# Stick-breaking attention in a hybrid decoder layer: two heads at a time in plain float32, each on one half of the array, in place of one head at a time in split float32r

## The chip, the cores and the metric

The kernel runs on one core of a Trainium2 chip. The metric is the device time of one execution in microseconds. Three executions of the kernel before took 1371.71, 1368.38 and 1372.44 us; the median is 1371.71 us. One more execution was recorded by the profiler; all durations below come from that one.

## The reference

One layer of a decoder trunk, 1024 tokens of width 1024, everything in float32. What the change touches is the attention half: 8 heads of 64 features.

```python
h = _modulate(_rmsnorm(x, norm1_g[l]), sh1, sc1)
p = h @ w_in[l]                       # q, k, v (512 each) and u (512)
q = _rmsnorm(q, q_norm_g[l]); k = _rmsnorm(k, k_norm_g[l])   # per head
o_attn = _stick_breaking(q, k, v)
o_ssm = _s5(u, ...)
o = concatenate([_rmsnorm(o_attn, attn_out_g[l]), _rmsnorm(o_ssm, ssm_out_g[l])])
x = x + g1 * (o @ w_out[l])
h = _modulate(_rmsnorm(x, norm2_g[l]), sh2, sc2)
up = _causal_dwconv(h @ ffn_w_up[l], ffn_conv_w[l], ffn_conv_b[l])
x = x + g2 * ((gelu(gate) * val) @ ffn_w_down[l])

def _stick_breaking(q, k, v):         # for each query t and key s < t
    z = einsum('bhqd,bhkd->bhqk', q, k) / sqrt(64)
    log_1m = where(mask, log_sigmoid(-z), 0.0)
    tail = cumsum(log_1m, reverse=True) - log_1m
    w = where(mask, exp(log_sigmoid(z) + tail), 0.0)
    return einsum('bhqk,bhkd->bhqd', w, v)
```

The weight of key s is sigmoid(z) times the product of sigmoid(-z) over the keys between s and the query.

## The kernel before

The program has three phases. **Phase A** makes norm1 and the modulation, the input projection of `u`, the state-space half (`ssm_batch`), and q, k and v. **Phase B** is attention head by head, with the output projections laid between. **Phase D** is the gated MLP (`upps`, `dnps`).

*Order.* Instructions are written in the order of the code, and a scheduler then reorders them on each engine by a timeline that it works out itself, as far as buffers and dependences allow. Each engine then runs its list in order. Weight loads stand on TensorE too (PEld in the profile) and overlap with the matmuls ahead of them. Loads and stores are issued on SP's queue, the stores of q and k (`qk_d`) on ACT's.

*Split operands.* Most products are made in float32r, and an operand that must keep all its bits is split in two: a rounded copy (`hi`, `wh`) and the remainder (`lo`, `wl`), made by a subtraction. So a projection is three matmuls a block (L551 to L553, and L773 to L775 for the output projection `wops`).

*q, k and v (L591 to L647).* For each 128 tokens the projections leave a PSUM bank `o`; q and k are normalised, transposed on PE into the one bank `qkT` (L613), and copied by ACT into the first half of `hl` (rounded to float32r); DVE writes the remainder into the second half. Both halves go to DRAM, `qk_d[cix, r]`. v is split in the same way into `vt`, 64 columns of hi and 64 of lo a head, and goes to `v_d`. `hl` and `vt` share two buffers of 512 KB. `ada_back` (`ada_acc`, L67, and `adps`) runs between them: it makes the modulation rows for later from the `ada_raw` loads.

*Attention (`head`, L676).* A head has 8 query tiles of 128; tile i needs keys 0 to 128(i+1), cut into blocks of up to 512 (`zcuts`). `q1` holds hi over lo on the 128 rows, `q2` lo over hi, `k1` hi over lo, so that L694 and L695 give all four products with 128 rows each. L697 adds -1e30 to the diagonal block by a bfloat16 matmul of `nmask`. Then:

- ACT makes `nb` = sigmoid(-z/8) and `sig` = sigmoid(z/8) (L698, L699),
- DVE scans `nb` from the right as a running product (L700),
- POOL multiplies `sig` by the shifted `nb` (L702; helpers are recorded at L61),
- PE transposes the weights in groups of up to four into a bank `wT` (L707), of which there are TB = 3,
- ACT copies them as `wh` (L711), DVE subtracts to `wl` (L712, recorded at L61).

After two query tiles, L717 and L718 multiply `wh` and `wl` by `vsb` (hi and lo of v, 128 columns): 256 tokens, result in a bank `ops` of its own. Its two halves (v hi, v lo) are added: ACT copies one into `otmp` (L720), DVE adds (`oT`, L721).

*Fillers.* `after_tile` counts the attention work done, and where its share passes an entry of `marks` (L812) the next piece of the output projection of the state-space half is written into the program (`fillers`). The last head has the groups of query tiles in reverse order, and behind each the output projection of the attention half (`tail_proj`).

*State-space products.* The trace of before shows matmuls on half an array there. L488 (`vps`) writes alternately the lower and the upper 64 partitions of its result, by 64 weight columns each, from all 128 rows. The products `yps` (L506 to L514) go

```python
for pr_ in range(2):
    for q in range(4):
        # L512: 128 rows      L513, L514: the 64 rows s_ of half pr_ alone
```

The scheduler moves the first L512 and L513 of `pr_` = 1 to the front, so that on PE's list these three follow one another: L513 of `pr_` = 0, q = 3; L514 of `pr_` = 0, q = 3; L514 of `pr_` = 1, q = 0.

## Time and profile before

| what | value |
|---|---|
| median of three runs | 1371.71 us (1368.38 to 1372.44) |
| span of the profiled execution | 1365.3 us |
| instructions | 16015 |
| PE busy | 1261.6 us, 92% of the span |
| PEld busy (beside PE) | 1034.5 us, 76% |
| DVE busy | 953.0 us, 70% |
| POOL busy | 385.3 us, 28% |
| ACT busy | 375.6 us, 28% |

The profiled execution has no device time of its own beside its span; the median is 6.4 us above the span. Busy times are shares of the whole span, which has stages with different limits: q, k and v and the state space until about 338 us, attention from there to about 640 us, the MLP to the end. A matmul's row gives its start and a modelled end; matmuls are pipelined, so the duration is longer than the distance from start to start, and that distance is what one costs in a stream. Plain float32 matmuls leave two records each, float32r and bfloat16 ones a single record. "x4" in a row stands for four records run together.

### The profile page before, as it was taken

Reading aid. Unit: us, or ns where it says so; the run is one execution under the profiler, and the core shown is the slowest. Engines: PE = TensorE matmul, PEld = TensorE weight load, DVE = VectorE, ACT = ScalarE, POOL = GpSimd, SP = SyncE. Lnnn points to the kernel's source line nnn. Section 1 sums busy time; section 2 is a strip of 40 time slices with the busy share of each in tenths; the row PEclk is TensorE's granted clock in tenths of the full one; section 3 lists DMA queues with packets and bytes.
Section 4 is the critical chain, followed back from the end, with each engine's and each line's share of the span. In section 5 each row is a group of like instructions: output and inputs, shape, how many; then the busy total and the mean of one; then the engine's idle time right before and its main releaser. Section 6 shows DMA issues by size and latency. Waiting matters only on the chain.

```text
span 1365.3 us, 16015 instructions
## 1 busy us (share of the span) xinstructions
PE 1261.6 (92%) x5988; PEld 1034.5 (76%) x5988; DVE 953.0 (70%) x1465; ACT 375.6 (28%) x651; POOL 385.3 (28%) x369
## 2 busy tenths in 40 slices
PE   5979899898778996898999999999999999999998
PEld 4767778677557785676788888888888888888886
DVE  6999999873998889875775555455465655555555
ACT  5431233431765666444111101010101010101010
POOL 3562461530684449512130101111111111111100
PEclk9889889999889998898999999999999999999999
DMA  8452445657934663000620102020211111111103
GB/s 342 149 139 63 122 142 141 157 169 230 242 97 145 213 187 106 32 16 20 199 91 31 62 31 78 16 77 18 75 42 56 46 57 47 47 47 47 47 1 123
DMA packets 98264, 134.78 MB, mean 99 GB/s; under 512 B 33414, under 2 KB 66310, under 8 KB 97164
## 3 DMA queue, kind: packets, MB, share of 16 engines
q1 hardware_dynamic: 81292, 125.38, 29.5%
q10 hardware_dynamic: 16896, 8.39, 2.2%
q8 instruction: 47, 0.77, 0.2%
q14 instruction: 29, 0.24, 0.1%
HBM read 107.40 MB, written 25.17 MB: 97 GB/s over the span
## 4 chain that ended last, share of the span: by engine, by line
PE 64%; DVE 20%; DMA 7%; issue 3%; POOL 2%; ACT 2%; SPq 1%; DVEq 0%; ACTq 0%; POOLq 0%
PE upps L916 11%; PE upps L917 11%; PE upps L918 11%; PE dnps L1004 6%; PE dnps L1005 6%; PE dnps L1003 6%; DVE ada_acc L67 3%; DMA ada_raw<-in_ada_r_dram 3%; DVE nb L700 2%; PE wops L773 2%; PE wops L774 1%; PE wops L775 1%; POOL sig L61 1%; DVE st L61 1%; DMA x<-in_x_dram 1%
## 5 line engine op out<-in xcount | busy, mean ns | idle before, releaser
L916 PE MATMUL upps<-h2hi,uphi 128*128 128x512 f32 x704 | 275.5, 391 | 2.3 <-DVE cv L67 2.0
L917 PE MATMUL upps<-h2lo,uphi 128*128 128x512 f32 x704 | 274.6, 390 | 0.2 <-DVE h2lo L61 0.2
L918 PE MATMUL upps<-h2hi,uplo 128*128 128x512 f32 x704 | 274.4, 390 | 0.0
L953 ACT ACTIVATE cv<-upps,cols_sb 128x1024 f32<-128x1024 f32 x44 | 53.2, 1209 | 500.3 <-PE upps L918 500.3
L916 PEld LDWEIGHTS upps<-h2hi,uphi 128*128 128x128 f32 x704 | 132.4, 188 | 30.8 <-issue 2.8
L917 PEld LDWEIGHTS upps<-h2lo,uphi 128*128 128x128 f32 x704 | 132.4, 188 | 28.1 <-DVE h2lo L61 0.5
L918 PEld LDWEIGHTS upps<-h2hi,uplo 128*128 128x128 f32 x704 | 132.4, 188 | 27.6 <-issue 0.2
L61 DVE TENSOR_TENSOR uplo<-upraw,uphi 128x1024 fp32r<-128x1024 f32 x44 | 55.5, 1262 | 127.1 <-POOL uphi L161 127.1
L1004 PE MATMUL dnps<-wdlo,ahi 128*128 128x512 f32 x352 | 137.0, 389 | 0.9 <-DVE wdlo L61 0.9
L1003 PE MATMUL dnps<-wdhi,ahi 128*128 128x512 f32 x352 | 136.6, 389 | 0.6 <-POOL wdhi L161 0.6
L1005 PE MATMUL dnps<-wdhi,alo 128*128 128x512 f32 x352 | 136.9, 389 | 0.0
L161 POOL TENSOR_SCALAR uphi<-upraw 128x1024 fp32r<-128x1024 f32 x44 | 47.5, 1080 | 281.1 <-PE upps L917 200.0
L61 DVE TENSOR_TENSOR xs<-dnps,xs 128x512 f32<-128x512 f32 x88 | 60.9, 692 | 86.9 <-PE dnps L1005 86.9
L67 DVE SCALAR_TENSOR_TENSOR cv<-upps,cols_sb,cv 128x1023 f32<-128x1023 f32 x88 | 112.4, 1278 | 11.6 <-ACT cv L953 10.9
L61 POOL TENSOR_TENSOR sig<-sig,nb 128x127 f32<-128x127 f32 (+3 forms) x64 | 98.2, 1542 | 70.5 <-DVE nb L700 47.4
L700 DVE TENSOR_TENSOR_SCAN nb<-nb 128x128 f32<-128x128 f32 (+3 forms) x64 | 105.8, 1667 | 8.0 <-ACT nb L698 7.6
L67 DVE SCALAR_TENSOR_TENSOR ada_acc<-ada_raw,c_sb,ada_acc 128x256 f32<-128x256 f32 (+1 forms) x97 | 74.2, 779 | 24.5 <-DMA ada_raw<-in_ada_r_dram 21.2
L551 PE MATMUL qkvp<-w_hi,hhi 128*128 128x512 f32 x192 | 78.5, 410 | 3.4 <-DVE qssq L604 2.9
L552 PE MATMUL qkvp<-w_lo,hhi 128*128 128x512 f32 x192 | 78.5, 409 | 0.6 <-POOL w_lo L61 0.6
L553 PE MATMUL qkvp<-w_hi,hlo 128*128 128x512 f32 x192 | 78.0, 406 | 0.0
L1004 PEld LDWEIGHTS dnps<-wdlo,ahi 128*128 128x128 f32 x352 | 66.1, 188 | 15.0 <-DVE wdlo L61 1.3
L1003 PEld LDWEIGHTS dnps<-wdhi,ahi 128*128 128x128 f32 x352 | 65.9, 188 | 14.7 <-POOL wdhi L161 1.0
(240 smaller groups left out, 2370.7 us busy)
## 6 DMA issues: line engine op xcount, KB each, us to landing
upraw<-in_w_up_dram SPq DMA_DIRECT2D x44, 512.0 KB, 3.2
ada_raw<-in_ada_r_dram SPq DMA_DIRECT2D x48, 256.0 KB, 2.8
wdraw<-in_w_down_dram SPq DMA_DIRECT2D x22, 512.0 KB, 3.8
ada_raw<-in_ada_a_dram SPq DMA_DIRECT2D x8, 1024.0 KB, 9.3
qk_d<-hl ACTq DMA_DIRECT2D x32, 256.0 KB, 2.8
q<-qk_d SPq DMA_DIRECT2D x32, 256.0 KB, 5.7
w_raw<-in_w_qkv_dram SPq DMA_DIRECT2D x24, 256.0 KB, 3.9
xt<-in_x_dram SPq DMA_DIRECT2D x8, 512.0 KB, 5.5
```

The source lines that it names most:

```text
L61: eng.tensor_tensor(out=out, in0=a, in1=b, op=op)
L67: dve.scalar_tensor_tensor(out=out, in0=a, scalar=s, in1=b, op0=op0, op1=op1)
L551: pe.matmul(o, lhsT=lh, rhs=his[k], start=(k == 0), stop=False)
L552: pe.matmul(o, lhsT=lh, rhs=los[k], start=False, stop=False)
L553: pe.matmul(o, lhsT=ll, rhs=his[k], start=False, stop=(k == NK - 1))
L700: dve.tensor_tensor_scan(out=nb[:, 0:n][:, ::-1], data0=nb[:, 0:n][:, ::-1], data1=nb[:, 0:n][:, ::-1], initial=1.0, op0=MUL, op1=ALU.bypass)
L916: pe.matmul(o, lhsT=hi[:, k, :], rhs=rh, start=(k == 0), stop=False)
L917: pe.matmul(o, lhsT=hi[:, k, :], rhs=rl, start=False, stop=False)
L918: pe.matmul(o, lhsT=lo[:, k, :], rhs=rh, start=False, stop=(k == NK - 1))
L1003: pe.matmul(o, lhsT=hi[:, a], rhs=whi[:, b], start=(i == 0), stop=False)
L1004: pe.matmul(o, lhsT=hi[:, a], rhs=wlo[:, b], start=False, stop=False)
L1005: pe.matmul(o, lhsT=lo[:, a], rhs=whi[:, b], start=False, stop=(i == len(ops) - 1))
```

## The change

Two heads are taken at a time, and q, k, v and the weights stay plain float32 without a split. q and k of the pair lie on the 128 rows, head 0 on rows 0 to 63 and head 1 on rows 64 to 127, so a score matmul uses 64 rows of the array. In the value product each head uses 64 columns and all 128 rows, and the two heads' results lie in the two halves of one bank. The mask is now made of two bfloat16 matmuls a head on 64 rows each (`msel`, `mrow`), whose tables `mask_tables` makes in phase A. `wT` has two banks in place of three, z four in place of two; `ops` has no bank of its own and shares the two of `wops` (`mm`). Copies out of `wT` go to ACT for head 0 and to DVE for head 1. The marks end at 0.75 in place of 0.875. The diff also removes comments, which is left out here.

```diff
-    qk_d = dram.tile([2, 2, 512, 1024], F32, name="qk_d")
+    qk_d = dram.tile([2, 512, 1024], F32, name="qk_d")
-    v_d = dram.tile([1024, 8, 128], F32, name="v_d")
+    v_d = dram.tile([1024, 512], F32, name="v_d")
...
+    def mask_tables():
+        for r in range(2):
+            c = slice(r * 64, r * 64 + 64)
+            o = slice((1 - r) * 64, (1 - r) * 64 + 64)
+            pool.memset(msel[r][:, o], 0.0)
+            tt(pool, msel[r][:, c], ident_b[:, 0:64], ident_b[:, 64:128], ADD)
+            twice = const.tile([128, 2, 64], BF16, name=f"mtw{r}")
+            pool.tensor_copy(twice, ident_b[:, c].unsqueeze(1).to_broadcast([128, 2, 64]))
+            ps = psU.tile([128, 512], F32, tag="aux", name="mps2")
+            pe.matmul(ps[:, 0:128], lhsT=twice.rearrange("p a b -> p (a b)"), rhs=nmask, start=True, stop=True)
+            act.activation(out=mrow[r], in_=ps[:, 0:128], func=AF.Copy)
...
-    TB, ZB, MB = 3, 2, 2
+    TB, ZB, MB = 2, 4, 2
...
-                hl = stg.tile([128, 2, 512], F32R, tag="hl", name="hl", bufs=2)
+                hl = stg.tile([128, 512], F32, tag="hl", name="hl", bufs=3)
                 if cix == 0:
-                    act.activation(out=hl[:, 0], in_=tp, func=AF.Copy, scale=gqk)
-                    stt(hl[:, 1], tp, gqk, hl[:, 0].bitcast(F32), MUL, SUB)
+                    act.activation(out=hl, in_=tp, func=AF.Copy, scale=gqk)
                 else:
-                    act_copy(hl[:, 0], tp)
-                    tt(dve, hl[:, 1], tp, hl[:, 0].bitcast(F32), SUB)
-                for r in range(2):
-                    act.dma_start(out=qk_d[cix, r].rearrange("(a p) t -> p a t", p=128)[:, :, t * 128:(t + 1) * 128],
-                                 in_=hl[:, r].bitcast(F32).rearrange("p (a t) -> p a t", t=128))
+                    act_copy(hl, tp)
+                act.dma_start(out=qk_d[cix].rearrange("(a p) t -> p a t", p=128)[:, :, t * 128:(t + 1) * 128],
+                              in_=hl.rearrange("p (a t) -> p a t", t=128))
...
-    def head_load_qk(hd):
-        q1, q2, k1 = [qp.tile([128, 1024], F32R, tag=n_, name=n_, bufs=2) for n_ in ("q1", "q2", "k1")]
-        for dst, w, sw in ((q1, 0, 0), (k1, 1, 0), (q2, 0, 1)):
-            for r in range(2):
-                sp.dma_start(out=dst[r * 64:r * 64 + 64].bitcast(F32), in_=qk_d[w, r ^ sw, hd * 64:hd * 64 + 64, :])
-        return q1, q2, k1
+    def pair_load_qk(pr):
+        qk = [qp.tile([128, 1024], F32, tag=n_, name=n_, bufs=2) for n_ in ("q", "k")]
+        for w in range(2):
+            sp.dma_start(out=qk[w], in_=qk_d[w, pr * 128:(pr + 1) * 128, :])
+        return qk
...
-        vt = stg.tile([128, 8, 128], F32R, tag="hl", name="vt", bufs=2)
-        act.activation(out=vt[:, :, 0:64], in_=o, func=AF.Copy)
-        tt(dve, vt[:, :, 64:128], o, vt[:, :, 0:64].bitcast(F32), SUB)
-        vlast = sp.dma_start(out=v_d[t * 128:(t + 1) * 128], in_=vt.bitcast(F32))
+        vt = stg.tile([128, 512], F32, tag="hl", name="vt", bufs=3)
+        act.activation(out=vt, in_=o, func=AF.Copy)
+        vlast = sp.dma_start(out=v_d[t * 128:(t + 1) * 128], in_=vt)
...
-    def head(hd, stk, groups, after_tile, after_group):
+    def pair(pr, stk, groups, after_tile, after_group):
...
+            wts = [[ap_.tile([128, 4, 256], F32, tag="wt", name="wt", bufs=6) for _ in range((ns + 3) // 4)] for h in range(2)]
...
-                    here[0] = pe.matmul(z[:, 0:cn], lhsT=q1[:, lq], rhs=k1[:, c0:c0 + cn], start=True, stop=False)
-                    pe.matmul(z[:, 0:cn], lhsT=q2[:, lq], rhs=k1[:, c0:c0 + cn], start=False, stop=not last)
+                    for h in range(2):
+                        here[0] = pe.matmul(z[h][:, 0:cn], lhsT=q[hs[h], lq], rhs=k[hs[h], c0:c0 + cn], start=True, stop=not last)
                     if last:
-                        pe.matmul(z[:, cn - 128:cn], lhsT=ident_b, rhs=nmask, start=False, stop=True)
+                        for r in range(2):
+                            for h in range(2):
+                                pe.matmul(z[h][:, cn - 128:cn], lhsT=msel[r][hs[h]], rhs=mrow[r][hs[h]], start=False, stop=(r == 1))
...
-                    act.activation(out=wh[:, 0:jn, cs_], in_=tv, func=AF.Copy)
-                    tt(dve, wl[:, 0:jn, cs_], tv, wh[:, 0:jn, cs_].bitcast(F32), SUB)
+                        if h == 0:
+                            act.activation(out=wv, in_=tv, func=AF.Copy)
+                        else:
+                            dve.tensor_copy(wv, tv)
...
-            o = psZ.tile([128, 512], F32, tag="o", name="ops", bufs=1)
+            o = psM.tile([128, 512], F32, tag="mm", name="ops", bufs=MB)
             for s in range(ns):
-                pe.matmul(o[:, 0:256], lhsT=vt[:, s, :], rhs=whs[s // 4][:, s % 4, :], start=(s == 0), stop=False)
-                pe.matmul(o[:, 0:256], lhsT=vt[:, s, :], rhs=wls[s // 4][:, s % 4, :], start=False, stop=(s == ns - 1))
-            tmp = ap_.tile([64, 256], F32, tag="otmp", name="otmp")
-            act.activation(out=tmp, in_=o[64:128, 0:256], func=AF.Copy)
-            tt(dve, oT[h * 64:(h + 1) * 64, pr, g * 256:(g + 1) * 256], o[0:64, 0:256], tmp, ADD)
+                for h in range(2):
+                    pe.matmul(o[hs[h], 0:256], lhsT=vt[:, s, hs[h]], rhs=wts[h][s // 4][:, s % 4, :], start=(s == 0), stop=(s == ns - 1))
+            act.activation(out=oT[:, pr, g * 256:(g + 1) * 256], in_=o[:, 0:256], func=AF.Copy)
...
-    marks = [a + (b - a) * j / n for a, b, n in ((0.02, 0.14, 22), (0.14, 0.80, 24), (0.80, 0.875, 12)) for j in range(n)]
+    marks = [a + (b - a) * j / n for a, b, n in ((0.02, 0.12, 22), (0.12, 0.69, 24), (0.69, 0.75, 12)) for j in range(n)]
```

How the scheduler's order moves is shown at two places. Before, TensorE's order in the middle of the attention stage has the scores of one head (L694, L695), the mask (L697) and then a piece of the output projection (`wops`); a number behind a name tells buffers apart.

```order
L694 MATMUL z_4138<-k1_3769,q1_3767 128x512
L695 MATMUL z_4138<-k1_3769,q2_3768 128x512
L697 LDWEIGHTS ident_b_74
L697 MATMUL z_4138<-nmask_76,ident_b_74 128x128
L773 MATMUL wops_4043<-wohi_3195,ohi_3899 128x512
```

In TensorE's order after the change, in the same stage, the scores of head 0 (`z_4245`) and of head 1 (`z_4246`) come one after the other, with masks between, and then the value products of the halves (`ops`); k and q are the pair's, and z's name tells the head.

```order
L707 MATMUL z_4245<-k_3635,q_3634 128x512
L711 LDWEIGHTS msel0_81
L711 MATMUL z_4245<-mrow0_83,msel0_81 128x128
L711 LDWEIGHTS msel1_82
L711 MATMUL z_4245<-mrow1_84,msel1_82 128x128
L707 MATMUL z_4246<-k_3635,q_3634 128x512
L711 LDWEIGHTS msel0_81
L711 MATMUL z_4246<-mrow0_83,msel0_81 128x128
L711 LDWEIGHTS msel1_82
L711 MATMUL z_4246<-mrow1_84,msel1_82 128x128
L735 MATMUL ops_4063<-wt_3936,vsb_3097 64x256
L735 MATMUL ops_4063<-wt_3934,vsb_3097 64x256
```

So the scheduler put the masks of head 0, which the code writes behind the scores of both heads, ahead of the scores of head 1. A little earlier in the same order, transposes (L723) stand between the two heads' scores as well.

```order
L707 MATMUL z_4208<-k_3635,q_3634 128x384
L711 LDWEIGHTS msel0_81
L711 MATMUL z_4208<-mrow0_83,msel0_81 128x128
L711 LDWEIGHTS msel1_82
L711 MATMUL z_4208<-mrow1_84,msel1_82 128x128
L723 MATMUL wT_4037<-ident_66,sig_4011 128x128 x4
L707 MATMUL z_4209<-k_3635,q_3634 128x384
L711 LDWEIGHTS msel0_81
L711 MATMUL z_4209<-mrow0_83,msel0_81 128x128
L711 LDWEIGHTS msel1_82
L711 MATMUL z_4209<-mrow1_84,msel1_82 128x128
L723 MATMUL wT_4043<-ident_66,sig_4011 128x128 x4
```

The full-array transposes part the two half-array blocks here. Counted over the whole order of the stage, of 48 pairs of score blocks (18,432 columns a head) 21 have the heads side by side (9,344 columns), 15 have only masks between (4,736) and 12 have other work between (4,352); the value products stand in 31 runs, and full-array and half-array shapes change places 154 times.

DVE's order before, in the late part of the attention stage, has the subtractions for `wl`, the additions for `oT` and the scans of one head (named `SCALAR_TENSOR_TENSOR nb` in this listing) between each other.

```order
L61 TENSOR_TENSOR wl_4894<-wT_4954,wh_4892 128x4x128
L61 TENSOR_TENSOR wl_4996<-wT_5009,wh_4995 128x128
L700 SCALAR_TENSOR_TENSOR nb_5082<-nb_5082 128x512
L61 TENSOR_TENSOR wl_4996<-wT_5034,wh_4995 128x2x128
L61 TENSOR_TENSOR oT_3067<-ops_4961,otmp_4978 64x256
L61 TENSOR_TENSOR wl_5048<-wT_5061,wh_5047 128x3x128
L700 SCALAR_TENSOR_TENSOR nb_5117<-nb_5117 128x640
```

After the change, in the middle of the stage, DVE's order has copies out of `wT` for head 1 and the scans of the two heads in pairs.

```order
L729 COPY wt_3787<-wT_3896 128x4x128
L716 SCALAR_TENSOR_TENSOR nb_4013<-nb_4013 128x1024
L67 SCALAR_TENSOR_TENSOR x1_3838<-wops_3844,sinv_3133,x1_3838 128x512
L729 COPY wt_3788<-wT_3902 128x2x128
L716 SCALAR_TENSOR_TENSOR nb_4014<-nb_4014 128x1024
L716 SCALAR_TENSOR_TENSOR nb_4122<-nb_4122 128x128
L716 SCALAR_TENSOR_TENSOR nb_4123<-nb_4123 128x128
L716 SCALAR_TENSOR_TENSOR nb_4154<-nb_4154 128x256
L716 SCALAR_TENSOR_TENSOR nb_4155<-nb_4155 128x256
```

Of the evacuations of `wT`, head 0's are gone from DVE; `oT` is written by ACT.

## Rows read from the trace of the kernel before

**Rows 1.** The head of the profile's page.

```profile
span 1365.3 us, 16015 instructions
```

**Rows 2.** Busy time by stage: the stretch (us) and its length, then busy us (x instructions) of PE, PEld, DVE, ACT and POOL, the granted clock of TensorE as a share of full speed, the DMA engines' mean busy share and GB/s.

```profile
100.00:310.00 210.00, 195.13 (x1045) 158.23 (x1044) 190.57 (x359) 61.92 (x98) 79.66 (x66) 0.92 0.48 132
310.00:338.00 28.00, 24.41 (x108) 19.86 (x106) 9.19 (x13) 3.00 (x5) 1.05 (x6) 0.95 0.77 230
338.00:640.00 302.00, 250.80 (x1364) 205.11 (x1364) 262.04 (x396) 181.61 (x395) 156.21 (x153) 0.91 0.42 122
640.00:1366.00 726.00, 717.30 (x3154) 591.60 (x3152) 403.82 (x416) 80.47 (x72) 95.95 (x89) 1.00 0.17 58
```

**Rows 3.** The chain of work that ended last, shares by line: first of the stretch 100 to 338 us, then of 356 to 600 us.

```profile
by line: DMA ada_raw<-in_ada_r_dram 14.6%; DVE ada_acc L67 8.3%; issue 5.6%; DVE R L497 4.8%; DVE dtm L61 4.7%; DMA v_d<-vt 4.3%; PE qkvp L551 4.1%; PE qkvp L553 4.0%; PE qkvp L552 4.0%; DVE ctmp L61 2.8%; PE yps L512 2.7%; PE yps L513 2.5%
...
by line: DVE nb L700 12.8%; POOL sig L61 7.8%; issue 7.2%; PE wops L773 6.5%; DMA x<-in_x_dram 6.2%; DVE wl L61 6.2%; PE wops L774 5.8%; PE wops L775 5.6%; PE wT L707 5.2%; PE ops L718 4.1%; PE ops L717 3.9%; DMA x_d<-x 3.7%; DVE otot L754 
```

**Rows 4.** PE's waits from 350 to 600 us: who waits for whom, total us, how often, the longest. The sig rows at L61 are POOL's products, the wl and oT rows at L61 DVE's subtractions and additions.

```profile
PE wT L707 <- POOL sig L61: 11.8, 7, 4.9
PE ops L718 <- DVE wl L61: 8.3, 6, 2.8
PE wT L707 <- DVE wl L61: 4.2, 7, 1.2
...
PE ops L717 <- DVE oT L61: 2.8, 3, 1.5
```

**Rows 5.** Groups of instructions from 338 to 640 us on DVE and on ACT: line, engine, operation, out<-in, shapes and count, then busy us and mean ns of one, then the idle time before them and what ended it.

```profile
L61 DVE TENSOR_TENSOR wl<-wT,wh 128x512 fp32r<-128x512 f32 (+2 forms) x96 | 49.5, 543 | 3.2 <-ACT wh L711 2.9
...
L61 DVE TENSOR_TENSOR oT<-ops,otmp 64x256 f32<-64x256 f32 x32 | 13.2, 412 | 1.8 <-ACT otmp L720 1.3
...
L711 ACT ACTIVATE wh<-wT 128x512 fp32r<-128x512 f32 (+2 forms) x96 | 44.8, 495 | 39.6 <-PE wT L707 26.0 <-PE ops L717 12.5 <-issue 0.5
...
L720 ACT ACTIVATE otmp<-ops 64x256 f32<-64x256 f32 x32 | 12.2, 382 | 12.5 <-PE ops L718 12.0
```

**Rows 6.** The tiles `hl` and `vt`: their instructions on DVE (shortest/median/longest ns, from when to when), and of those who wait for the tile or stand waiting ahead of it: the waiter, total us, how often. The line of `qkT` is PE's wait for DVE to free that bank, the line of `v_d<-vt` ACT's wait for a buffer, the line of `adps` PE's wait.

```profile
L67 DVE SCALAR_TENSOR_TENSOR hl<-qkT,gqk,hl x8: 739/746/751, 154.6 to 229.7; 128x512 fp32r<-128x512 f32 x8
L61 DVE TENSOR_TENSOR hl<-qkT,hl x8: 678/683/686, 244.3 to 301.8; 128x512 fp32r<-128x512 f32 x8
...
  PE qkT L613: 5.5, 2
...
L61 DVE TENSOR_TENSOR vt<-qkvp,vt x8: 681/688/692, 302.4 to 336.7; 128x512 fp32r<-128x512 f32 x8
...
  DMA v_d<-vt: 21.5, 5
...
  PE adps L575: 3.6, 1
```

**Rows 7.** PE's timeline in the attention stage: start (us), duration (us), engine, line, operation, out<-in, array used, shape and count. Two stretches, at 446.9 and at 450.4 us.

```profile
446.90 0.28 PE L717 MATMUL ops<-wh,vsb 128*128 128x256 f32 x1
447.02 0.28 PE L718 MATMUL ops<-wl,vsb 128*128 128x256 f32 x1
...
450.37 0.23 PE L697 MATMUL z<-nmask,ident_b 128*128 128x128 bf16 x1
450.41 0.36 PE L717 MATMUL ops<-wh,vsb 128*128 128x256 f32 x1
```

**Rows 8.** The chain in order of time, in the q and k stage: start (us), duration (us), what. The projection (L553) has single float32r matmuls of 512 columns; `gps` and `adps` are plain float32 (L522: 128 columns, a record of one of the two passes each; L571: 512 columns); `vps` is the product in column halves.

```profile
202.25 0.23 PE qkvp L553
...
205.00 1.34 PE gps L522 x12
206.34 0.86 PE adps L571 x2
...
213.42 1.90 PE vps L488 x32
```

**Rows 9.** PE's timeline of the products in row halves, columns as in rows 7; `64*128` is the part of the array used. The L513 at 141.31 and the L514 at 141.54 belong to one half of the rows, the L514 at 141.33 to the other.

```profile
139.84 0.49 PE L512 MATMUL yps<-U,W 128*128 128x128 f32 x2
140.26 0.48 PE L513 MATMUL yps<-S,W 64*128 64x128 f32 x2
140.58 0.38 PE L514 MATMUL yps<-S,W 64*128 64x128 f32 x2
140.90 0.49 PE L512 MATMUL yps<-U,W 128*128 128x128 f32 x2
141.31 0.37 PE L513 MATMUL yps<-S,W 64*128 64x128 f32 x1
141.33 0.37 PE L514 MATMUL yps<-S,W 64*128 64x128 f32 x1
...
141.54 0.48 PE L514 MATMUL yps<-S,W 64*128 64x128 f32 x3
```

**Rows 10.** The same view where four L513 records stand between two projections of 512 columns.

```profile
234.21 0.39 PE L552 MATMUL qkvp<-w_lo,hhi 128*128 128x512 f32 x1
234.53 0.49 PE L513 MATMUL yps<-S,W 64*128 64x128 f32 x4
234.95 0.50 PE L553 MATMUL qkvp<-w_hi,hlo 128*128 128x512 f32 x1
```

**Rows 11.** A part of the last quarter of the attention stage, columns as in rows 2.

```profile
540.00:570.00 30.00, 21.80 (x137) 19.02 (x136) 29.01 (x40) 18.57 (x43) 26.39 (x21) 0.84 0.06 18
```

More of the change, by code (lines that the diff above doesn't have):

```diff
@@ L108, in hybrid_layer_kernel @@
     pool.affine_select(out=nmask, in_=nmask, pattern=[[-1, 128]], compare_op=ALU.is_gt, fill=-1e30, base=0, channel_multiplier=1)
+    msel = [const.tile([128, 128], BF16, name=f"msel{r}") for r in range(2)]
+    mrow = [const.tile([128, 128], BF16, name=f"mrow{r}") for r in range(2)]
     c_sb = const.tile([128, 8], F32, name="c_sb")
@@ L416, in hybrid_layer_kernel @@
     tt(dve, gqk, gq_sb, gk_sb, MUL)
+    mask_tables()
     pn.release()
@@ L850, in tail_proj @@
         rsqrt(small, n2inv[:, 2 * g:2 * g + 2], ssq, 2)
[L852 to L854 removed]
+    stk = (stk0, pair_load_v(0))
+    for pr in range(NPAIR):
         nxt = {}
[L856 removed]
+        last_pair = pr == NPAIR - 1
         def after_tile(i):
[L859 removed]
+            if not last_pair:
                 if i == 0:
[L861 to L862 removed]
+                    nxt["p"] = (after_v(pair_load_qk, 1) if pr == 0 else pair_load_qk(pr + 1), pair_load_v(pr + 1))
+            state["w"] += 2 * (i + 2)
             while state["q"] < len(marks) and marks[state["q"]] <= state["w"] / (44.0 * NH):
@@ L866, in after_tile @@
                     next(fill, None)
-        if last_head:
+        if last_pair:
             run_all(fill)
             load_xacc()
-        head(hd, stk, (3, 2, 1, 0) if last_head else range(4), after_tile, tail_stats if last_head else lambda g: None)
+        pair(pr, stk, (3, 2, 1, 0) if last_pair else range(4), after_tile, tail_stats if last_pair else lambda g: None)
         stk = nxt.get("p")
@@ L894, in norm2 @@
     def norm2(g):
-        xn = [qp.tile([128, 1024], F32, tag=n_, name="xn", bufs=2) for n_ in ("q1", "q2")]
+        xn = [qp.tile([128, 1024], F32, tag=n_, name="xn", bufs=2) for n_ in ("q", "k")]
         for j in range(2):
```

64 lines of the change are left out of this document (28 added, 36 removed).

## The prediction

> **What bounds the kernel now.** I read the page's head first and then the stages. The profiled execution spans 1365.3 us; the median of the three runs shown is 1371.7, so 6.4 us lie around the span, and I keep them as they are [rows 1]. The table of stages comes next [rows 2]: from 640 us to the end PE is busy 717 of 726 us at full clock, and nothing of the change runs there. The change sits in 100 to 640 us. While q, k and v are made (100 to 310) PE is busy 195 and DVE 191 of 210 us, so neither alone decides. From 310 to 338 the DMA engines carry it (share 0.77). In the attention stage, 338 to 640, DVE is busy 262 of 302 us and PE 251, at a mean granted clock of 0.91: by the two levels, 18% of the stage was at 1.2 GHz. The chain of waits for 356 to 600 agrees [rows 3]: scans on DVE lead with 12.8%, POOL's products follow with 7.8%, and no line holds the stage alone. PE's own waits there [rows 4] are 11.8 us for POOL's products, 12.5 us for the `wl` subtractions on DVE (8.3 before the second product, 4.2 before a transpose that wants a PSUM bank) and 2.8 us for `oT`. So attention is held by DVE first and by PE close behind, and every term has to be put on one of these two.
>
> **What comes off DVE and ACT.** The 96 `wl` subtractions (49.5 us) and 32 `oT` additions (13.2 us) go; 48 copies out of PSUM come [rows 5]. No DVE copy of that kind is in the trace. From below half of ACT's `wh` copies of the same data prices the 48 at 22.4 us, from above half of `wl` at 24.8; I take 24. Net on DVE: 24 - 62.7 = -38.7 us, 262 to 223. ACT loses half of `wh` (22.4) and `otmp` (12.2) and gains 16 `oT` copies at 0.38 (6.1); it was busy 182 of 302, so this shortens no end by itself. POOL loses 32 of its 64 memsets, and is not the end either.
>
> Before attention, DVE loses eight `hl` at 746 ns, eight at 683 and eight `vt` at 688, 16.9 us in all [rows 6]. What ended last from 100 to 338 us was the `ada_raw` DMAs first, with 14.6% [rows 3], so I count the wait that surely goes: PE's 5.5 us for `hl` to free the single `qkT` bank, now freed by ACT's copy. Ends 0 and 16.9, taken 6. In 310 to 338, `v_d` writes halve (8 x 512 KB to 8 x 256 KB), the first q and k loads fall from 1.5 to 1 MB, `vt` has three buffers and no DVE step. ACT waited 21.5 us for `v_d` buffers, but PE, which streams the projections, lost only some 3.6 us to it, at the end, before `adps`: taken 3, ends 0 and 6. The shorter loads later (8 issues on SP's queue for 48) I count at 0, since they are prefetched one head ahead. `mask_tables` adds two PE products and a few small POOL and ACT steps before 338 us, where POOL is busy 80 of 210: 0, or some 2 us without that cover.
>
> **What PE pays.** The sizes first. From start to start a float32r matmul of 256 columns takes 0.12 us and the bfloat16 mask 0.04 [rows 7]; one of 512 columns takes 0.23 [rows 8]. A plain float32 matmul is two records: the two of 512 columns take 0.86 us, and twelve of 128 take 1.34 (0.11 each) [rows 8]. So for one 512 block of scores of two heads: before 4 x 0.23 = 0.92, after 2 x 0.86 = 1.72 one behind the other, or 0.86 if the halves run at once. The whole change hangs on whether they do, and the trace of before has both shapes, in the state-space stage. Column halves: 32 records of `vps`, alternating between 64-column halves, take 1.90 us, 0.06 each against 0.11 for the full array [rows 8]. Row halves: four `L513` records (two matmuls, one on each half of the rows) are through, shape change and all, 0.42 us after they begin, just as the two records of one full `L512` are (139.84 to 140.26) [rows 9, 10].
>
> Scores: four pairs need 18,432 columns, 36 blocks of 512: 33.1 us before. In PE's order 9,344 columns have the two heads side by side, 4,736 have only masks between, and 4,352 have transposes or output products between and cannot overlap. That a matmul overtakes one that stands between is seen: `L514` of one row half starts at 141.33, 0.02 us after `L513` of the other, although that other half's `L514`, which starts at 141.54, stands between the two in PE's order [rows 9]. So 27.5 blocks x 0.86 + 8.5 x 1.72 = 38.3 us: +5. If masks blocked it, 18.25 x 0.86 + 17.75 x 1.72 = 46.2: +13. The Trainium skill (TensorE: Matmul & The Clock Gate, Part 3, The mechanism) says that matmuls start and end strictly in program order, and only weight loads are pulled ahead; by that the masks would block, and the sum would be 8 us higher. The row at 141.33 differs, and I follow the row.
>
> Values: 320 x 0.12 = 38.4 us before; 80 pairs x 0.43 = 34.4 after, plus about 20 odd runs (the order cuts them into 31) that each leave half a pair, 0.21, alone: 38.6. That is 0; without overlap it would be +30. Masks: 64 full become 128 half ones; by 0.04 each +3, by 0.11 each, the record of 128 columns, +11; taken 3.
>
> Changes of the tile shape are new in this stage: PE's order has 154 of them. Price: three matmuls `L512`, `L513`, `L514` come round in 1.06 us (139.84 to 140.90), of which six records of 0.11 are 0.64; the two shape changes in it cost 0.21 each [rows 9]. Around the `L513` excursion the first part of it shows alone: 0.23 us after 234.21 the projection is through, and `L513` begins at 234.53, 0.09 later [rows 10]. Between 154 x 0.09 = 14 and 154 x 0.21 = 32; the round has the same kinds of weights, so 32.
>
> PE in attention: +5 + 0 + 3 + 32 = +40 us (ends +15 and +56), against -39 on DVE.
>
> **The sum.** PE's 251 us become 291 of 302. Of the 251, up to 27 are stretch of the lower clock (18% of 302 us at half speed); I estimate that half of it goes when PE is denser, giving 278. Idle was 51. The 15 us for `wl` and `oT` go, half of the 12 behind POOL's products (whose inputs are DVE's scans), and part of the rest is filled by having more work queued: 20 remain. 278 + 20 = 298, -4; I take -5. Transposes have two banks for three, and `ops` shares the two banks of `wops`; half of the evacuations now leave by ACT alone, so I count these within the 20. Total: 1365.3 - 6 - 3 - 5 = 1351, plus 6.4 = 1358.
>
> **Rivals.**
> - *Full relief, 1334 us.* PE loses the whole stretch (251 - 27 + 40 = 264) with 10 idle: stage 274, -28; with -10 before it 1371.7 - 38 = 1334. For it: DVE at 223 would no longer hold anyone. Against: PE works in order through scans, products and transposes.
> - *Masks hold the second head, 1366 us.* As worked out above, PE pays 8 more. For it: 15 of 48 blocks are ordered so; against it is the row at 141.33. The rule of the Trainium skill named above is this rival.
> - *Nothing arrives, 1371 us.* Halves overlap, but what DVE saves lies beside the `ada_raw` transfers and PE's load, and attention pays on PE just what it saves. The equal terms 40 and 39 speak for it; the waits of PE for `wl` against.
> - *PE becomes the bound, 1390 us.* PE has 291 us to do in the stage, and if its idle stays as now the stage is 342. It decides as soon as idle plus lost clock exceeds the saving: 291 + idle > 302 + 9, an idle of 20 at the present clock. The place is the last quarter, which has no filler left (marks end at 0.75 for 0.875): in 540 to 570 PE is busy 21.8 of 30 us at clock 0.84 though DVE is at 29 [rows 11]. With half of the idle that is above 20 left standing and the clock as now, 291 + 36 = 327, +25 - 6: 1390.
>
> **How the numbers follow.** 0.3%, about 4 us, is what a measurement of this kernel tells from no change. Forecast 0.42, with its own range 1345 to 1370 (0.39 faster, 0.03 same); full relief 0.16, faster; masks 0.10, half faster and half same; nothing 0.10, same; PE the bound 0.22, slower. Faster 0.60, same 0.18, slower 0.22. The range reaches from a little below full relief, 1328, to a little above the slower rival, 1396.
>
> **What would show it.** Of after: `z` records of the two heads starting within 0.02 us of each other, also where masks stand between; `ops` at some 0.21 per record pair; PE waiting for `wl` gone and DVE near 223 us in the stage; gaps of 0.1 and exposed weight loads at each shape change; PE above 92% busy with the clock above 0.93. It is wrong if halves run one behind the other (stage +50), if a shape change costs little (stage shorter by up to 18), or if PE stands idle over 30 us for POOL's products or for the two `wT` banks.

## The result and the profile after

The changed kernel takes 1386.8 us (median of four runs, 1383.52 to 1390.65) against 1371.26 for the kernel before: ratio 1.0125, 95% interval 1.0092 to 1.0157. The forecast was 1358 us, faster. The profiled execution is the slowest of the four (1390.65 us), so differences in it are a little larger than those of the medians.

The page's head and the stages of the profile after, in the columns of [rows 2]:

```profile
span 1388.9 us, 15784 instructions
...
100.00:310.00 210.00, 198.06 (x1041) 160.72 (x1040) 175.05 (x345) 61.92 (x99) 82.20 (x66) 0.90 0.41 111
310.00:338.00 28.00, 28.00 (x143) 22.65 (x143) 8.11 (x13) 6.00 (x18) 3.13 (x10) 1.00 0.60 186
338.00:640.00 302.00, 251.49 (x1312) 161.73 (x1307) 222.49 (x274) 141.15 (x301) 156.76 (x111) 0.89 0.24 82
640.00:1389.00 749.00, 736.77 (x3244) 605.89 (x3242) 420.00 (x454) 90.55 (x91) 101.92 (x97) 1.00 0.17 57
```

Between 338 and 640 us DVE does 222 us of work where it did 262; the forecast was 223. But the attention stage no longer ends at 640, so the two rows do not hold the same work. It is compared better from the first score product to where the MLP's up-projection goes on with `h2lo` (a single product of it can stand a few us earlier). The same view for the kernel before:

```profile
337.90:621.30 283.40, 236.32 (x1299) 194.99 (x1300) 250.71 (x372) 173.55 (x380) 150.53 (x145) 0.91 0.44 128
```

and for the changed kernel:

```profile
334.40:642.20 307.80, 257.29 (x1351) 165.87 (x1351) 227.15 (x290) 144.89 (x314) 158.89 (x113) 0.89 0.24 83
```

The stage grew by 24 us. PE is busy 21 us longer; its idle time, length less busy time, is 50.5 us where it was 47.1. It was to fall to 20. DVE's work falls from 250.7 to 227.2 us, by 23.6 and not by the 38.7 forecast. The subtractions and additions are gone and the 48 copies take 25.3 us (24 were counted), but other instructions take longer, the 64 scans above all (line, shapes and count, busy us and mean ns of one, idle time before them, before and then after):

```profile
L700 DVE TENSOR_TENSOR_SCAN nb<-nb 128x128 f32<-128x128 f32 (+3 forms) x64 | 105.8, 1667 | 8.0 <-ACT nb L698 7.6 <-POOL sig L61 0.2 <-POOL wh L684 0.2
```

```profile
L716 DVE TENSOR_TENSOR_SCAN nb<-nb 128x128 f32<-128x128 f32 (+7 forms) x64 | 114.0, 1810 | 13.9 <-ACT nb L713 13.2 <-POOL sig L61 0.5
```

PE's waits after, from 350 to 640 us, as in [rows 4]:

```profile
PE ops L735 <- DVE wt L729: 11.8, 3, 7.8
PE nps L770 <- DVE otot L769: 11.3, 7, 3.5
PE wT L723 <- DVE wt L729: 7.7, 6, 1.8
PE wops L789 <- POOL wolo L61: 5.2, 1, 5.2
PE wT L723 <- ACT wt L727: 4.1, 6, 1.6
PE wops L788 <- POOL wohi L165: 3.0, 1, 3.0
```

The waits for `wl`, `oT` and for POOL's products `sig` are gone from this list, and the whole list still comes to some 47 us, where the list of before (350 to 617 us) comes to 44. The wait list names who came last; it does not say why the instructions stood in that order. The timeline does. PE from 403 to 428 us (start, duration, line, as in [rows 7]; in brackets the idle time before and what ended it):

```profile
403.34 0.44 PE L723 MATMUL wT<-ident,sig 128*128 128x128 f32 x2 [1.78 <-DVE wt L729]
...
408.38 0.52 PE L723 MATMUL wT<-ident,sig 128*128 128x128 f32 x3 [1.68 <-DVE wt L729]
408.83 2.17 PE L707 MATMUL z<-k,q 64*128 64x512 f32 x8
410.55 0.66 PE L711 MATMUL z<-mrow,msel 64*128 64x128 bf16 x4
414.22 1.22 PE L788 MATMUL wops<-wohi,ohi 128*128 128x512 f32 x2 [3.01 <-POOL wohi L165]
420.68 0.79 PE L789 MATMUL wops<-wolo,ohi 128*128 128x512 f32 x1 [5.24 <-POOL wolo L61]
...
422.12 0.63 PE L790 MATMUL wops<-wohi,olo 128*128 128x512 f32 x1
422.74 5.73 PE L735 MATMUL ops<-wt,vsb 128*64 128x256 f32 x32
```

and the last copies of the weights that this `ops` multiplies (query tiles 6 and 7 of the first pair), on ACT and on DVE:

```profile
393.28 0.60 ACT L727 ACTIVATE wt<-wT 128x512 f32<-128x512 f32 x1
...
397.50 0.68 DVE L729 COPY wt<-wT 128x512 f32<-128x512 f32 x1
```

All weights lie ready at 398.2. The 32 records of the value product begin at 422.7, 24.5 us later. Between, PE stands idle for 11.7 us, 8.25 of it for POOL's `wohi` and `wolo`, with this product ready behind the output projection that waits. Both kinds write into the two banks `mm`. A piece of the output projection is a sum of 12 matmuls (four parts of the weights, three matmuls each), and it holds its bank until the last of them. In the same view from 387 us on, L788 to L790 have 24 records up to 422.12, so two such sums: one begins at 387.59, the other at 398.39, and both end behind 421 us, because the last part of their weights comes from POOL only then:

```profile
411.95 2.22 POOL L165 TENSOR_SCALAR wohi<-woraw 128x1024 fp32r<-128x1024 f32 x1
...
416.84 3.78 POOL L61 TENSOR_TENSOR wolo<-woraw,wohi 128x1024 fp32r<-128x1024 f32 x1
```

So from 398.39 on both banks were taken by sums that waited for weights, and the value product had none.

### The profile page after: what moved, and what is told of

It is laid out like the page before. It is cut to its first block, busy times and chain, and to the rows that moved or that the text cites. A ratio compares the mean times of both kernels' runs of the same rounds, so it can differ in the third digit from the quotient of the medians.

```text
span 1388.9 us, 15784 instructions
## 1 busy us (share of the span) xinstructions
PE 1287.1 (93%) x6054; PEld 1008.7 (73%) x6054; DVE 912.7 (66%) x1361; ACT 348.5 (25%) x589; POOL 397.7 (29%) x343
## 3 DMA queue, kind: packets, MB, share of 16 engines
q1 hardware_dynamic: 74444, 112.80, 25.3%
## 4 chain that ended last, share of the span: by engine, by line
PE 67%; DVE 21%; DMA 5%; issue 3%; POOL 2%; ACT 2%; SPq 0%; DVEq 0%; POOLq 0%; ACTq 0%
PE upps L930 11%; PE upps L931 11%; PE upps L932 11%; PE dnps L1018 6%; PE dnps L1019 6%; PE dnps L1017 6%; DVE ada_acc L67 4%; DVE nb L716 3%; PE ops L735 3%; DMA ada_raw<-in_ada_r_dram 2%; PE wops L788 2%; PE wops L789 2%; PE wops L790 2%; PE z L707 1%; DVE dtm L61 1%
## 5 line engine op out<-in xcount | busy, mean ns | idle before, releaser
L61 DVE TENSOR_TENSOR uplo<-upraw,uphi 128x1024 fp32r<-128x1024 f32 x44 | 56.9, 1292 | 124.0 <-POOL uphi L165 123.9
L61 POOL TENSOR_TENSOR sig<-sig,nb 128x127 f32<-128x127 f32 (+7 forms) x64 | 105.9, 1670 | 72.4 <-DVE nb L716 31.1
L716 DVE TENSOR_TENSOR_SCAN nb<-nb 128x128 f32<-128x128 f32 (+7 forms) x64 | 114.0, 1810 | 13.9 <-ACT nb L713 13.2
L61 DVE TENSOR_TENSOR xs<-dnps,xs 128x512 f32<-128x512 f32 x88 | 60.9, 692 | 86.9 <-PE dnps L1019 86.9
L1017 PEld LDWEIGHTS dnps<-wdhi,ahi 128*128 128x128 f32 x352 | 65.9, 188 | 14.6 <-POOL wdhi L165 1.0
```

The source lines that it names most:

```text
L61: eng.tensor_tensor(out=out, in0=a, in1=b, op=op)
L716: dve.tensor_tensor_scan(out=nb[h][:, 0:n][:, ::-1], data0=nb[h][:, 0:n][:, ::-1], data1=nb[h][:, 0:n][:, ::-1], initial=1.0, op0=MUL, op1 ...
L1017: pe.matmul(o, lhsT=hi[:, a], rhs=whi[:, b], start=(i == 0), stop=False)
```

## The experiments

### Does the busy time of one engine decide?

Two runs take the kernel before and change one engine's load; a third does it in the changed kernel. `b_nowl` takes DVE's subtractions away; the result lacks the remainder of the weights.

```diff
-                    tt(dve, wl[:, 0:jn, cs_], tv, wh[:, 0:jn, cs_].bitcast(F32), SUB)
+            wls = whs
```

> The kernel before without the 96 wl subtractions on DVE (49.5 us of its busy time); both value products take wh, so the remainder of the weights is left out of the result and PE's matmuls stay the same in number and size. If DVE holds the attention stage, as the prediction had it, PE's idle of 47 us falls to about 25 and the time to about 1348 us. If PE's idle comes from the length of the chain (scores, sigmoids, scan, product, transposes) where no filler stands, the time falls by 10 us at most, to 1361 or more.

Measured: 1368.9 us against 1368.2, ratio 0.9993 (0.9973 to 1.0013). The stage in the same view, between the same two products:

```profile
337.70:622.10 284.40, 235.74 (x1298) 194.78 (x1299) 212.28 (x276) 173.29 (x380) 144.46 (x116) 0.90 0.44 128
```

DVE is busy 38 us less and the stage is 1 us longer. PE's idle is 48.7 us. So DVE's load did not hold the stage of the kernel before: the relief on which the forecast rested is worth nothing by itself there. It was not tried alone in the changed kernel.

`b_halfmask` makes the masks in column halves:

```diff
-    pe.matmul(z[:, cn - 128:cn], lhsT=ident_b, rhs=nmask, start=False, stop=True)
+    for hc in range(2):
+        cc = slice(hc * 64, hc * 64 + 64)
+        pe.matmul(z[cc, cn - 128:cn], lhsT=ident_b[:, cc], rhs=nmask, start=False, stop=True)
```

> The kernel before with each of the 64 masks in two column halves of 64: the same sums, 64 matmuls more and 128 changes of the tile shape more. If a change of shape costs about 0.15 us, as the gaps in the trace after the change read, PE's busy time grows by 128 x 0.15 = 19 us and the time by 10 to 19 us, to 1381 to 1390. If it costs nothing that matters, it is within 4 us of 1371.

Measured: 1369.4, ratio 1.0003 (0.9985 to 1.0022).

```profile
338.90:625.00 286.10, 246.59 (x1362) 195.89 (x1363) 254.33 (x372) 174.09 (x380) 148.68 (x145) 0.93 0.43 127
```

PE is busy 10.3 us longer, at most 0.08 for each of the 128 changes of shape, and its idle falls from 47.1 to 39.5: idle takes up 7.6 of the 10.3. `a_rows0` takes the overlap of the score halves away in the changed kernel (scores and masks of both heads come from head 0's rows; head 1's scores are left out). Of the two edited lines, the scores:

```diff
-    pe.matmul(z[h][:, 0:cn], lhsT=q[hs[h], lq], rhs=k[hs[h], c0:c0 + cn], ...)
+    pe.matmul(z[h][:, 0:cn], lhsT=q[hs[0], lq], rhs=k[hs[0], c0:c0 + cn], ...)
```

> The changed kernel with the scores and masks of both heads from rows 0 to 63, that is head 0's, so that the halves can't run at once; the second head's scores are left out. At most 36 blocks x 0.86 us = 31 us more of PE's time, and 64 masks. If PE is the bound of the stage, the time grows by 20 to 31 us, to 1407 or more; if the chain is, PE's idle takes it up and the time grows by less than 10 us.

Measured: 1394.8, 8 us more than the changed kernel.

```profile
334.90:648.60 313.70, 279.57 (x1352) 177.28 (x1352) 225.66 (x290) 147.80 (x315) 155.15 (x113) 0.91 0.24 82
```

PE is busy 22 us longer than in the changed kernel and the stage grows by 6; idle falls to 34. PE is no plain bound either. The expectation's two bounds were 20 and 10; this is the second case.

### Buffers and fillers

`a_bufs6` gives `sig` and `nb` six buffers, `a_oldmarks` puts the old `marks` back.

```diff
-                sig = [ap_.tile([128, 1024], F32, tag="sig", name="sig", bufs=4) for h in range(2)]
+                sig = [ap_.tile([128, 1024], F32, tag="sig", name="sig", bufs=6) for h in range(2)]
...
-    marks = ... ((0.02, 0.12, 22), (0.12, 0.69, 24), (0.69, 0.75, 12))
+    marks = ... ((0.02, 0.14, 22), (0.14, 0.80, 24), (0.80, 0.875, 12))
```

> The changed kernel with six buffers each for sig and nb in place of four, so that three pairs of query tiles are under way in place of two. If PE's idle of 48 us in the stage stayed because the pairs halve the look-ahead, it falls by 10 to 20 us, to about 1372. If PE's extra work and the chain itself decide, it is within 4 us of 1387.

> The changed kernel with the marks of the kernel before (to 0.875 in place of 0.75; what is left at the start of the last pair is then written there at once). If the earlier end of the fillers leaves PE idle, the time falls by 5 to 10 us, to about 1379. If not, it is within 4 us of 1387.

Measured: 1389.1 and 1385.1, both within 2.5 us of the changed kernel. Look-ahead in `sig` and `nb` is not what is missing, and the marks alone are not either.

### Which part of the change?

`e_v` keeps the split scores of before and changes only the values, two heads at a time; it has the PSUM banks of before, marks to 0.75, and for want of room a single buffer for the second head's q and k. `e_v4` is the same with the changed kernel's banks. `a_banks` is the changed kernel with the banks of before. The score lines of `e_v` against the change, and the banks of `a_banks`:

```diff
-    here[0] = pe.matmul(z[h][:, 0:cn], lhsT=q[hs[h], lq], rhs=k[hs[h], c0:c0 + cn], start=True, stop=not last)
+    q1, q2, k1 = qks[h]
+    here[0] = pe.matmul(z[h][:, 0:cn], lhsT=q1[:, lq], rhs=k1[:, c0:c0 + cn], start=True, stop=False)
+    pe.matmul(z[h][:, 0:cn], lhsT=q2[:, lq], rhs=k1[:, c0:c0 + cn], start=False, stop=not last)
...
-    TB, ZB, MB = 2, 4, 2
+    TB, ZB, MB = 3, 2, 2
...
-            o = psM.tile([128, 512], F32, tag="mm", name="ops", bufs=MB)
+            o = psZ.tile([128, 512], F32, tag="o", name="ops", bufs=1)
```

> The value part of the change alone: two heads at a time, v and the weights plain float32, value products in column halves, copies out of wT on ACT and DVE, marks to 0.75; scores as before (split float32r on the full array, full masks), and the PSUM banks as before (wT three, z two, ops one of its own). The second head's q and k have one buffer, for want of room. If the score part (row halves, half masks and their changes of shape) is what the changed kernel loses by, it is at about 1371 us or below; if taking heads in pairs or the value part loses, at 1380 to 1390.

> The same with the PSUM banks of the changed kernel (wT two, z four, ops in the two banks of wops). If the banks matter, it is over 5 us slower than with the banks of before; if not, within 4 us of it.

> The changed kernel with the PSUM banks of before (wT three, z two, ops one of its own). PE waited 11.8 us for the two wT banks and 11.8 us ahead of ops. If the banks hold the stage, the time falls by 8 to 15 us, to about 1376; if not, it is within 4 us of 1387, or slower, as two z banks hold a single pair of score blocks.

Measured: 1379.3, 1393.9 and 1379.4; the first and the last miss their ranges by under 1 us. The banks are worth 14.6 us with the one kind of scores and 7.4 with the other. What the score part is worth, to which most of the forecast's working went, stays open. `e_v` and `a_banks` are equal, but with the changed kernel's banks the paired scores are 7 us faster (1386.8 against 1393.9), and in `e_v` PE waits for the loads into its single buffer, which the changed kernel does not have (waits from 333 to 632 us):

```profile
PE z L698 <- DMA k1b<-qk_d: 13.1, 3, 6.5
```

A loss of about 10 us against before was left, and the fillers were the suspect: the last pair, a quarter of attention, has none. In `a_banks_late` and `e_v_late` the marks run to 0.84, and the rest is written behind the first group of the last pair by `last_group`, which is called behind each of its groups. `b_late` does the same in the kernel before (marks to 0.92). `b_early` does the opposite there: marks to 0.75, and the rest ahead of the last two heads. The edit of `a_banks_late`, without the marks:

```diff
-        if last_pair:
-            run_all(fill)
-            load_xacc()
+        def last_group(g):
+            if g == 3:
+                run_all(fill)
+                load_xacc()
+            tail_stats(g)
```

> The changed kernel with the PSUM banks of before (1379 us), and the fillers run on through the first group of query tiles of the last pair (marks to 0.84, the rest behind that group in place of ahead of the pair). If what is still lost against before, some 10 us, is that the last quarter of attention has no filler work where before it was the last eighth, the time falls by 6 to 10 us, to about 1371. If it is the extra work on PE, or the pairs themselves, it stays within 4 us of 1379.

> The kernel before with the marks of the changed kernel (to 0.75) and the rest of the fillers written ahead of the last two heads in place of the last one. If the missing filler work in the last quarter is the cause, the time grows by 6 to 12 us, to about 1378; if not, it is within 4 us of 1369.

> The value part alone with the PSUM banks of before (1379 us) and the fillers through the first group of the last pair. If the fillers are the cause of the rest: 1369 to 1373, and lower than before if the saving on DVE then counts; if the pairs are: within 4 us of 1379.

> The kernel before with its fillers drawn on through the first group of the last head (marks to 0.92). If filler work beside the last tiles is what counts, it is some 3 to 6 us faster than before, 1363 to 1366; if before was already placed well, within 3 us of 1369.

Measured: `a_banks_late` 1370.7, ratio 1.0015 (0.9997 to 1.0033), so banks and later fillers bring the changed kernel back to the kernel before. `b_early` 1375.7, ratio 1.0038 (1.0016 to 1.0061): the kernel before loses about 5 us by ending its fillers early, slightly less than the 6 expected. But `e_v_late` is 1382.8, 3.5 above `e_v` (the two intervals overlap, and PE waits 9.2 us for the same loads), and `b_late` 1374.1, about 4 above before, where faster or equal was expected. Later fillers are no rule; of these three arrangements they help in one.

### Which bank?

`a_late` has the later fillers and the changed kernel's banks. `a_t3_late` gives wT its third bank, `a_ops_late` gives `ops` a bank of its own; both take it from z, which keeps three, and have the later fillers too. `a_dve_late` is `a_banks_late` with the second head's product on DVE.

```diff
-                    tt(pool, sig[h][:, 0:n - 1], sig[h][:, 0:n - 1], nb[h][:, 1:n], MUL)
+                    tt(dve if h else pool, sig[h][:, 0:n - 1], sig[h][:, 0:n - 1], nb[h][:, 1:n], MUL)
```

> The changed kernel with nothing but its fillers drawn on through the first group of the last pair (marks to 0.84), and its own PSUM banks. Banks and fillers together took it from 1387 to 1371, the banks alone to 1379. If the two add up, it is at 1376 to 1381; if the fillers help only once the banks are free, at 1384 or more.

> Late fillers, three wT banks, three z banks, and ops still in the two banks of wops. If the third wT bank is what helped, it is at about 1371 to 1373; if the bank for ops is, at 1376 or more.

> Late fillers, two wT banks, three z banks, and a bank for ops alone. If the bank for ops is what helped, it is at about 1371 to 1373; if the third wT bank is, at 1376 or more.

> Late fillers, the PSUM banks of before, and the product sig x nb of the second head on DVE in place of POOL: 32 products leave POOL (about 53 of its 106 us) and come to DVE, which has lost 39 us to the change. If the chain of scan and product in each step holds the stage (PE waited 15.9 us for POOL's products in the run with late fillers), the time falls by 6 to 15 us below 1371, to 1356 to 1365, and beats both kernels. If PE's work or the fillers hold it, it is within 4 us of 1371.

Measured: 1386.9, 1404.1, 1370.8 (ratio 1.0025, 1.0004 to 1.0046) and 1377.5. The bank for `ops` is worth 16 us, the third wT bank is none of it: with both (`a_banks_late`) the time is the same 1370.7. Why `a_t3_late` is 17 us slower than `a_late` is open: three z banks do no harm where `ops` has its own (`a_ops_late`), and a third wT bank without the loss of a z bank was not tried. The rival that I had set up in place of DVE's load, the chain of scan and product, is not borne out: half of POOL's products on DVE cost 7 us instead of saving 6 or more. But this run puts them on the engine that makes the scans, so it does not show that a shorter chain would be worth nothing.

The last two runs each change that one thing: in the changed kernel (`a_ops`, z keeps three banks), which is shown, and the other way round in the kernel before (`b_mm`: `ops` moves into `mm`, nothing else, and one bank stays empty).

```diff
-    TB, ZB, MB = 2, 4, 2
+    TB, ZB, MB = 2, 3, 2
...
-            o = psM.tile([128, 512], F32, tag="mm", name="ops", bufs=MB)
+            o = psZ.tile([128, 512], F32, tag="o", name="ops", bufs=1)
```

> The changed kernel with one thing put back: ops has a bank of its own again (taken from z, which keeps three); wT two banks, marks to 0.75 as in the change. If the shared banks are the cause, the product of the first pair's last group follows its last copy within a few us, where the changed kernel has it 22 us later, and the time falls to 1370 to 1377. If the bank helps only with the later fillers, it is at 1380 or more.

> The kernel before with one thing taken from the change: ops in the two banks of wops, nothing else (one of the eight banks stays empty). If the shared banks are the cause, it loses what the changed kernel lost, 8 to 18 us, 1377 to 1387. If they only hurt with heads in pairs, it is within 4 us of 1369.

Measured: `a_ops` 1377.3 (1371.5 to 1385.0), ratio 1.0065 (1.0040 to 1.0090), 9.5 us below the changed kernel. `b_mm` 1397.0, ratio 1.0199 (1.0178 to 1.0220): that single edit costs the kernel before 27 us, more than the whole change and more than the 8 to 18 expected. The stage in `a_ops`, and then, from the timelines of DVE and PE, the first pair's last group there: the copy that ends last and the product:

```profile
324.80:616.40 291.60, 268.58 (x1362) 168.67 (x1362) 227.86 (x292) 146.80 (x316) 159.39 (x113) 0.94 0.25 88
```

```profile
385.63 0.66 DVE L729 COPY wt<-wT 128x512 f32<-128x512 f32 x1
...
385.92 1.95 PE L735 MATMUL ops<-wt,vsb 128*64 128x256 f32 x16
387.80 0.33 PE L723 MATMUL wT<-ident,sig 128*128 128x128 f32 x1
...
388.29 1.94 PE L735 MATMUL ops<-wt,vsb 128*64 128x256 f32 x14
```

The product begins even before the last copy is through (the first 16 records need the earlier ones), where the changed kernel's began 24.5 us behind. PE's idle in the stage is 23.0 us, and its clock 0.94. This profile is the fastest execution of `a_ops` (1371.51 us), and attention begins in it 9.6 us earlier than in the changed kernel's, so what the bank is worth is read from the medians. The idle does not hang on that one execution: in `a_ops_late`, whose profile is at its median, it is 19.1 us, and in `a_banks`, where `ops` has its own bank too, 18.8 (the stages in this order):

```profile
329.30:618.40 289.10, 270.00 (x1360) 169.89 (x1361) 225.14 (x292) 146.79 (x314) 155.28 (x113) 0.91 0.25 89
```

```profile
333.90:635.60 301.70, 282.88 (x1362) 175.63 (x1362) 221.47 (x292) 148.36 (x316) 148.13 (x113) 0.90 0.24 85
```

In `b_mm` it goes the other way:

```profile
335.00:635.50 300.50, 240.31 (x1276) 196.44 (x1276) 253.17 (x362) 172.04 (x378) 141.70 (x145) 0.88 0.42 121
```

with 60.2 us of idle, and the end shows the same delay. Its last subtraction in DVE's timeline, and its second product in the view of one line from 565 us on (shortest/median/longest ns, from when to when):

```profile
573.84 0.42 DVE L61 TENSOR_TENSOR wl<-wT,wh 128x256 fp32r<-128x256 f32 x1
```

```profile
L718 PE MATMUL ops<-wl,vsb x15: 274/283/415, 564.8 to 611.2; 128*128 128x256 f32 x15
```

The last weights are ready at 574.3 and multiplied at 611.2; in the kernel before they are ready at 567.7 and multiplied at 574.9, in the same two views (from 560 us on):

```profile
567.08 0.62 DVE L61 TENSOR_TENSOR wl<-wT,wh 128x128 fp32r<-128x128 f32 x2
```

```profile
L718 PE MATMUL ops<-wl,vsb x12: 279/415/579, 561.7 to 574.9; 128*128 128x256 f32 x12
```

The changed kernel has it there too: its last copy on DVE starts at 590.46, its last product at 617.6. What is shown is that the shared banks make a loss and that the products come late with them. That open sums hold both banks was counted at one place, 398 to 422 us of the changed kernel. How much of the loss goes that way, and how the scheduler comes to its order elsewhere, was not tried by itself.

Later fillers help `a_ops` as well: `a_ops_late` is 6.5 us below it. So in the changed kernel they are worth 6.5 to 8.7 us once `ops` has its own bank, and nothing before (`a_late`). No run beat the kernel before beyond its interval.

## Why the prediction was wrong, step by step

**The step that failed** is in the sum: "Idle was 51 [...] 20 remain", and in it "`ops` shares the two banks of `wops`; [...] so I count these within the 20". I saw the edit and gave it no price. The idle stayed at 50.5. With a bank of its own for `ops` it is 23.0, nearly the 20 forecast: the sharing is worth some 27 us of PE's idle in the profile, 9.5 us of the median, 16 with later fillers, and 27 us in the kernel before. That is not the whole miss of 29 us. Of it the bank takes 9.5 us and the early end of the fillers another 6.5 (`a_ops` to `a_ops_late`); the remaining 13 are the gain itself, which no run showed.

**The second failure** is the reading of the stage as "held by DVE first". Over the same work DVE saved 23.6 us, not the 39 worked out, and `b_nowl` saved 38 for no gain. A busy engine, 250 of 283 us, and a chain of waits led by its scans did not make it the one that decides. Had the banks been left alone, the forecast would still have been too low: `a_banks` is 0.76% above before. Its idle is 18.8 us, as forecast, but PE is busy 46.6 us longer than before, where the sum had 27 (291 less half of the clock's stretch, against 251). Even in `a_ops_late` the stage is 5.7 us longer than before and not 5 shorter: PE's busy time is up by 33.7 and its idle down by 28.0, where 31 was forecast.

**The PE terms** were right in kind. Both halves run at once, over masks too, but less often than counted. By the starts of the single records in the traces (two heads within 0.03 us of each other), 60% of the score columns do so in the changed kernel, where 76% were counted (27.5 of 36 blocks), and only 28% in `a_ops` and 20% in `a_banks`, which have three and two banks for z in place of four. By the prediction's own prices this makes the scores 43, 53 and 56 us where 38 were counted, an estimate. So the bank that `ops` gets from z has a price of its own; a bank for `ops` with four left for z was not tried. Here a 256-column block of both heads (four records), where PE's order has head 0's masks between the two heads, and a stretch with three changes of shape, both of the changed kernel:

```profile
346.70 0.71 PE L707 MATMUL z<-k,q 64*128 64x256 f32 x4
347.24 0.28 PE L711 MATMUL z<-mrow,msel 64*128 64x128 bf16 x4
...
442.33 0.39 PE L790 MATMUL wops<-wohi,olo 128*128 128x512 f32 x1
442.65 1.95 PE L735 MATMUL ops<-wt,vsb 128*64 128x256 f32 x16
444.53 0.77 PE L723 MATMUL wT<-ident,sig 128*128 128x128 f32 x5
445.22 1.13 PE L707 MATMUL z<-k,q 64*128 64x512 f32 x4
446.28 0.50 PE L788 MATMUL wops<-wohi,ohi 128*128 128x512 f32 x1
```

The masked block is through in 0.54 us, where one head after the other would need 0.86 (four records of 0.215). The rule that I had weighed (the Trainium skill, TensorE: Matmul & The Clock Gate, Part 3, The mechanism: starts strictly in program order) does not hold for matmuls on different rows in this row, and the rival built on it did not come. In [rows 9] the overtaken `L514` starts even later than I read: of the three records at 141.54 the first is the second pass of the `L514` of 141.33, and the overtaken one begins at 141.64. The conclusion is the same. The pair of 512 columns takes 1.06 where 0.86 were counted, with a change of shape; eight matmuls of the value product, four pairs, take 1.88 where 1.72 were counted, with another. A change is thus some 0.15 to 0.2 us at the gaps, and at most 0.08 over the 128 of `b_halfmask`, which are column halves of masks alone. By these the term is 12 to 31 us, so 32, at 0.21 for each, was at the upper end or above it. PE's busy time grew by 21 us, against 40 less half of the clock's stretch, 26.5; with most of the overlap of the scores lost (`a_banks`) it grew by 46.6.

**The clock** was to rise with a denser PE; it stayed, 0.91 before and 0.89 after, and so did the idle. In `a_ops`, with 23.0 us of idle, it is 0.94, but 0.91 in `a_ops_late` with 19.1 and 0.90 in `a_banks` with 18.8. So less idle did not bring a higher clock by itself.

**Ahead of attention** 9 us were counted and 3.5 came: the first score starts at 334.4 in place of 337.9. That is one execution: in runs with the same code ahead of attention it starts between 324.8 (`a_ops`) and 337.0 (`a_late`). PE's waits for `hl` and before `adps` [rows 6] are gone but for 0.2 us, yet the chain from 100 to 334 us is led as before by the `ada_raw` transfers (13.9%, 14.6 before). I read from this that the 6 us for `hl` lay beside them; no run tried it.

**The rivals.** "PE becomes the bound, 1390 us" has the right number, and its condition, that idle stays, came true; but its mechanism did not. 22 us more of PE's work cost 8 (`a_rows0`), and the idle had a cause that could be taken away, which that rival did not name. Its place, the last quarter without fillers, is part of the loss once `ops` has its own bank (8.7 us from `a_banks`, 6.5 from `a_ops`) and of nothing without it (`a_late`). The sign that the prediction named for itself, PE idle over 30 us for POOL's products or for the two `wT` banks, came as idle but not by these names: the list has 11.8 us for the `wT` copies, 8.2 for POOL's weights and none for its products.

## What to carry to other kernels

When a change frees or takes a buffer, price that edit like an instruction: ask which work on the same engine shares the buffer, how long each holds it and on what it waits meanwhile, and what lies ready behind it. Before counting an engine's saving as time, take that work away alone in the kernel before, as with `b_nowl`; high busy time and the first place in the chain of waits were no proof. And when idle time stays though its named waits are gone, look for instructions whose inputs were ready long before they ran. A kernel made to leave one part of a change out can bring a wait of its own, as the single buffer of `e_v` did: read its waits before comparing.

## What the runs showed of the hardware that was not expected

- Busy time on PE can grow without the time of the kernel: by 10.3 us in `b_halfmask` at equal time. And `a_banks`, where most scores run one head after the other over the two z banks, has PE busy some 25 us more than the changed kernel and is 7 us faster.
- Two plain float32 matmuls on opposite row halves start together although masks for one of them stand between (346.70), so the price of such an order is near that of the adjacent one: 0.54 us against 0.43 counted for two records at once.
